# The two attention-gate blocks as a Strassen pair, with P1 and P2 of a layer's first two pairs ahead of its token sums

## The chip, the core and the metric

One core of a Trainium2 chip. The metric is the device time of one execution in microseconds; three executions of the kernel before took 1616.82, 1615.01 and 1616.28 us, median 1616.28. TensorE (PE in the profile) multiplies, VectorE (DVE) and ScalarE (ACT) do elementwise work, GpSimd (POOL) a few small operations and the stores, and SyncE (SP) issues the loads.

## The reference

Two layers of a hybrid encoder on 512 tokens of width 2048, all in float32:

```python
h = rmsnorm(x, g_pre)
z = h @ w_in                       # 2048 -> 7184 columns
gq, gk, gv, gg, ga, aq, ak, av, ag = split_columns(z)
log_a = log_sigmoid(ga @ w_alpha + b_alpha) / 16
o_gla = rmsnorm(gla_chunk_causal(gq, gk, gv, log_a), g_gla) * silu(gg)
o_att = rmsnorm(chunk_band_attention(aq, ak, av, rel_bias), g_att) * silu(ag)
y = concatenate([o_gla, o_att]) @ w_out
x = x + rmsnorm(y, g_post)
```

`ag` and `gg` are the gates of the attention heads and of the GLA heads, 1024 columns each.

## The kernel before

**Products.** The weights lie in HBM as 18 blocks of 512 columns a layer (14 of `w_in`, four of `w_out`); a block is eight chunks of 128x1024 (two k-tiles of 128 rows by 512 columns). One chunk with its product is a `Job`. Every operand is split into a rounded high and a low part, and a product is high·high + high·low + low·high, so three matmuls. `Job.high` casts the chunk to `wh` on ACT (line 221), `Job.low` subtracts on DVE to get `wl` (line 226). The ring of `wh` has four buffers, that of `wl` three: DVE can be three jobs ahead of PE.

`std_gemm` (line 324) uses one chunk for all four token tiles: 24 matmuls of 128x512. `fast_gemm` (line 360) does a pair of blocks by seven Strassen-Winograd products P1 to P7, each on half of the tokens, half of the depth and one block's width: 28 jobs of 12 matmuls, 336 where two blocks by `std_gemm` take 384. The products need sums of weight chunks (DVE, lines 210, 213, 232) and sums of token operands: with A11, A12 (tokens 0 to 255, first and second half of the depth) and A21, A22 (tokens 256 to 511), S1 = A21-A22, S2 = S1-A11, S3 = A11-A21, S4 = A12+S2. P1 takes A11, P2 takes A12, P5 takes S1, P6 S2, P3 S4, P7 S3, P4 A22. `token_sums` makes the sums chunk by chunk, four 128x512 sums and four splits a chunk (lines 648 and 109/110), into four staging slots, stores them to HBM on the POOL queue, and each pair loads them again as `sa` (a ring of four).

**Order of a layer.** AG0 and AG1 (attention gate) by `std_gemm`; then the pairs GG (GLA gate), AV, QK01/QK23, QK45/QK67, GK/GQ, GV; then the output projection, two blocks standard and two as a pair (`W23`, `end=True`) whose P1 and P2 come first with P2 in its own PSUM banks. In layer 1 AG0 runs twice: tokens 0 to 255 first (lines 842 to 845), since the second half of the tokens is finished only after layer 0's last products, and then 256 to 511. Beside the products a list of tasks (`pump`, `Pace`) puts the rest into the program: preparing tokens, their norms, the sums.

**Preparing tokens.** `prep_chunk` scales a chunk of a half's tokens by `g_pre` (ACT/DVE lines 606 to 610) and splits it (109/110); in layer 1 PE first transposes it (593). `token_norms` sums the squares of the token rows on ACT (481), reduces on DVE (482), takes the power on POOL (468), and PE turns the result (549). In layer 0 the rows come from `x` on the SP queue (`load_row`, 500), behind weights and transposed columns; gates need them only at their evacuation. The kernel hands all this to a scheduler, which fixes the order on each engine; an engine takes its instructions in that order.

Of the kernel before, what the change touches and what calls it, by code (L numbers as in the profile page):

```python
# [16 lines left out]
P = 128  # L17
# [3 lines left out]
W = 512  # L21
# [14 lines left out]
def hybrid_trunk(  # L36
# [91 lines left out]
    CO = (0, 4, 1, 5, 2, 6, 3, 7)  # L128
    OO = (5, 4, 7, 6, 2, 3, 0, 1)
    PAIRS = ((GG0, GG1), (AV0, AV1), (QK01, QK23), (QK45, QK67), (GK, GQ), (GV0, GV1))  # L130
# [11 lines left out]
    PROD_END = products(C_END, "P1", "P2", "P5")  # L142
    PROD_END += middle(C_END) + products(C_END, "P7", "P4")
# [7 lines left out]
    class Job:  # L151
# [8 lines left out]
        def load(self):  # L160
# [3 lines left out]
            if k == "std":  # L164
                i = done["load"]
                if i == 0:
                    self.raw = rtile("raw")
                    load_columns(i, 0)
                    parts = w[self.l, b0, c].rearrange("p (k n) -> p k n", k=2)
                    for kk in range(2):  # L170
                        with tc.issue_after(last_load[0]):
                            last_load[0] = nc.sync.dma_start(self.raw[:, kk, :], parts[:, kk, :]).ins
                    load_columns(i, 1)
                elif i < NCH:
                    load_columns(i, 0)
                    self.raw = self.fetch(rtile("raw"), b0, c)
                    load_columns(i, 1)
                    if i == 1:
                        load_gate_columns(0)
                else:  # L180
                    self.raw = self.fetch(rtile("raw"), b0, c)
                if NCH - 2 <= i < NCH + 2:
                    half, j = divmod(i - NCH + 2, 2)
                    with tc.issue_after(last_load[0]):
                        rows[half, j] = load_row(half, j, x, nc.sync)
            elif k == "P1":
                p["H", c] = self.fetch(rtile("H"), b0, top)
            elif k == "P5":
                p["r", c] = self.fetch(rtile("raw"), b1, top)
            elif k == "P6":  # L190
                p["r", c] = self.fetch(rtile("raw"), b1, bottom)
            elif k == "P7":
                p["r", c] = self.fetch(rtile("raw"), b0, top)
            elif k == "P2" or k == "P4" and end:
                p["r", c] = self.fetch(rtile("raw"), b0, bottom)
            src = (so_d if end else sa_d)[self.l].get((LEFT.get(k), c))
            if src is not None:
# [4 lines left out]
        def high(self):  # L202
# [3 lines left out]
            else:  # L206
                h, r = p["H", c], p.get(("r", c))
                src = h if k in ("P1", "P5", "P6", "P4") else r
                if k in ("P5", "P6") or k == "P4" and self.b0 == W23[0]:
# [13 lines left out]
        def low(self):  # L223
# [6 lines left out]
            if self.kind == "P2" and self.b0 != W23[0]:  # L230
# [4 lines left out]
    for l in range(L):  # L235
        for _ in range(min(l, 1) + 1):
            stream += [Job(l, "std", c, AG0) for c in CO]
        stream += [Job(l, "std", c, AG1) for c in CO]
        for b0, b1 in PAIRS:
            pr = {}  # L240
# [3 lines left out]
        pr = {}  # L244
# [113 lines left out]
    roles = ["XY", "YX"]  # L358

    def fast_gemm(l, pair, consume, rate=0.0, skip=0, feature_major=False, after=None, end=False, scaled=True):  # L360
        b0 = pair[0]
        acc = {n: [ps_mm.tile([P, W], F32, tag="mm", name=nm("mm")) for _ in range(2)] for n in roles[0]}
        roles.reverse()
        target = {"P1": "X", "P5": "Y", "P6": "X", "P3": "Y", "P7": "X", "P2": "Y", "P4": "X"}
        starts = ["P1", "P5", "P2"]
        if end:
            target.update(P2="Z", P4="Y")
            starts.append("P4")
        prod = PROD_END if end else PROD
# [25 lines left out]
        def finished(k, t):  # L395
# [9 lines left out]
            elif k == "P4":  # L405
                consume(0, 1, t, x_, None)
# [1018 lines left out]
```

## Time and profile before

| | us |
|---|---|
| median of three runs | 1616.28 (1615.01 to 1616.82) |
| span of the profiled execution | 1614.0 |
| PE busy | 1604.6 (99%) |
| DVE busy | 1213.3 (75%) |
| ACT busy | 897.0 (56%) |
| bytes moved | 469.93 MB, 291 GB/s over the span |
| first product of the GG pair in layer 0 | at 99.3 |

The page gives the profiled execution by its span alone, from the first to the last instruction; 1614.0 is 2.3 under the median, and what lies around it is not shown. Time is worth something where PE would wait: a busy share of 75% on DVE is a mean over stages of which some leave it no slack. A duration in a row is longer than the distance between starts when an engine overlaps one instruction with the next.

### The profile page before, as it was taken

To read this page: it belongs to the slowest core of one execution; us is meant where nothing else is said; L and a number is where in the kernel's file an instruction comes from. 1 tells how busy PE (TensorE), PEld (TensorE's weight loads), DVE (VectorE), ACT (ScalarE), POOL (GpSimd) and SP (SyncE) were. 2 spreads that over 40 slices of the span, in tenths; PEclk is the share of its full clock that TensorE was granted. 3 is DMA by queue.
4 is the path that set the end of the run, shared out by engine and by line. 5 is a ranking of instruction groups with operands and counts; after the bars stand their busy time and mean duration, and the time that the engine had idled before them with its cause. 6 is when DMAs were issued, how large, how long until landed. Compare 5 with 4: busy or idle time off the path is not lost.

```text
span 1614.0 us, 24639 instructions
## 1 busy us (share of the span) xinstructions
PE 1604.6 (99%) x8914; PEld 1372.8 (85%) x8914; DVE 1213.3 (75%) x1566; ACT 897.0 (56%) x1492; POOL 164.2 (10%) x258
## 2 busy tenths in 40 slices
PE   9999999999999999999999999999999999999997
PEld 6888889999988877788888888899999888777886
DVE  7567776787877776678877676768778768866887
ACT  7545544457676534555774445445566765445553
POOL 1210000001101101310122100000001011013100
PEclk9999999999999999999999999999999999999999
DMA  9989786958868698998789897968588676979986
GB/s 373 357 296 335 274 319 221 312 179 292 297 215 292 209 345 284 339 361 304 284 299 341 301 331 268 319 226 300 183 314 294 212 271 235 360 239 353 370 304 236
DMA packets 150809, 469.93 MB, mean 291 GB/s; under 512 B 16444, under 2 KB 35524, under 8 KB 150688
## 3 DMA queue, kind: packets, MB, share of 16 engines
q1 hardware_dynamic: 128096, 390.05, 69.4%
q0 software_dynamic: 22016, 77.37, 12.4%
q8 instruction: 70, 1.15, 0.3%
q10 hardware_dynamic: 576, 0.95, 0.2%
q14 instruction: 51, 0.42, 0.1%
HBM read 396.16 MB, written 71.06 MB: 289 GB/s over the span
## 4 chain that ended last, share of the span: by engine, by line
PE 99%; DMA 0%; DVE 0%; ACT 0%; SPq 0%; DVEq 0%; POOLq 0%; issue 0%
PE mm L430 46%; PE mm L344 22%; PE mm L420 20%; PE ax L937 2%; PE ax L430 1%; PE ax L920 1%; PE ax L1103 1%; PE ax L1137 1%; PE ax L900 1%; PE ax L899 1%; PE ax L898 1%; PE ax L579 1%; PE ax L968 0%; PE ax L593 0%; PE ax L1165 0%; DMA raw<-in_w_dram 0%
## 5 line engine op out<-in xcount | busy, mean ns | idle before, releaser
L430 PE MATMUL mm<-wh,sa 128*128 128x512 f32 x1536 | 483.9, 391 | 0.0
L221 ACT CAST wh<-raw 128x1024 fp32r<-128x1024 f32 x255 | 268.9, 1056 | 246.0 <-PE mm L430 96.9
L226 DVE TENSOR_TENSOR wl<-raw,wh 128x1024 fp32r<-128x1024 f32 (+1 forms) x257 | 312.4, 1218 | 116.9 <-PE mm L430 36.3
L226 DVE TENSOR_TENSOR wl<-H,wh 128x1024 fp32r<-128x1024 f32 x224 | 273.4, 1222 | 117.4 <-PE mm L430 52.3
L221 ACT CAST wh<-H 128x1024 fp32r<-128x1024 f32 x224 | 234.9, 1052 | 216.9 <-PE mm L430 110.5
L430 PEld LDWEIGHTS mm<-wh,sa 128*128 128x128 f32 x1536 | 287.4, 188 | 60.4 <-issue 1.5
L430 PE MATMUL mm<-wl,sa 128*128 128x512 f32 x768 | 299.7, 390 | 0.0
L420 PE MATMUL mm<-sa,wh 128*128 128x256 f32 x1280 | 237.4, 286 | 0.0
L420 PEld LDWEIGHTS mm<-sa,wh 128*128 128x128 f32 x1280 | 199.8, 191 | 0.3
L430 PE MATMUL mm<-wh,a 128*128 128x512 f32 x576 | 187.2, 393 | 0.0
L420 PE MATMUL mm<-sa,wl 128*128 128x256 f32 x640 | 180.6, 283 | 0.0
L430 PEld LDWEIGHTS mm<-wl,sa 128*128 128x128 f32 x768 | 144.2, 188 | 29.7
L344 PE MATMUL mm<-wh,a 128*128 128x512 f32 x512 | 166.4, 393 | 0.1
L210 DVE TENSOR_TENSOR H<-H,raw 128x1024 f32<-128x1024 f32 x120 | 145.6, 1220 | 3.3 <-DMA raw<-in_w_dram 1.7
L468 POOL TENSOR_TENSOR sm<-sm,mhalf 128x4 f32<-128x4 f32 (+2 forms) x40 | 55.1, 1376 | 760.8 <-DVE sm L953 527.6
L430 PEld LDWEIGHTS mm<-wh,a 128*128 128x128 f32 x576 | 107.9, 188 | 24.7 <-issue 2.9
L420 PEld LDWEIGHTS mm<-sa,wl 128*128 128x128 f32 x640 | 122.3, 191 | 0.1
L344 PEld LDWEIGHTS mm<-wh,a 128*128 128x128 f32 x512 | 96.2, 188 | 21.9 <-issue 1.2
L430 PE MATMUL mm<-wl,a 128*128 128x512 f32 x288 | 112.5, 391 | 0.0
L344 PE MATMUL mm<-wl,a 128*128 128x512 f32 x256 | 100.7, 394 | 0.0
L420 PE MATMUL mm<-a,wh 128*128 128x256 f32 x512 | 94.9, 285 | 0.0
L344 PE MATMUL mm<-wh,sa 128*128 128x512 f32 x256 | 86.4, 397 | 0.0
(207 smaller groups left out, 2262.3 us busy)
## 6 DMA issues: line engine op xcount, KB each, us to landing
raw<-in_w_dram SPq DMA_DIRECT2D x319, 512.0 KB, 5.4
sa<-S SPq DMA_DIRECT2D x192, 512.0 KB, 4.8
H<-in_w_dram SPq DMA_DIRECT2D x56, 512.0 KB, 4.4
sa<-A SPq DMA_DIRECT2D x48, 512.0 KB, 6.7
S<-g POOLq DMA_DIRECT2D x32, 512.0 KB, 7.5
oS<-g POOLq DMA_DIRECT2D x32, 512.0 KB, 6.4
sa<-oS SPq DMA_DIRECT2D x32, 512.0 KB, 4.4
sg<-t POOLq DMA_DIRECT2D x32, 256.0 KB, 6.0
```

The costliest lines, as they stand in the source:

```text
L210: nc.vector.tensor_tensor(out=h, in0=h, in1=r, op=ALU.add)
L221: last_cast[0] = nc.scalar.copy(self.wh, src).ins
L226: last_low[0] = nc.vector.tensor_tensor(out=self.wl[:, kk, :], in0=self.src[:, kk, :], in1=self.wh[:, kk, :].bitcast(F32), op=ALU.subtract ...
L344: mm = nc.tensor.matmul(pss[o], a[:, part, t], rhs[:, kk, :], start=(i == 0 and kk == 0 and m == 0), stop=(i == n - 1 and kk == 1 and m == 2),
L420: nc.tensor.matmul(dst, lhs[:, kk, f], a[:, part, tok], start=(fresh and kk == 0 and m == 0 and ft % 2 == 0), stop=(c == c_last and kk == ...
L430: nc.tensor.matmul(out_ps[t], a[:, part, tok], rhs[:, kk, :], start=(fresh and kk == 0 and m == 0), stop=(c == c_last and kk == 1 and m == ...
L468: return nc.gpsimd.tensor_tensor(out=out_r, in0=v, in1=mhalf[:, : v.shape[-1]], op=ALU.pow).ins
L579: mm = nc.tensor.matmul(gate_ps[l][g : g + 32, half * 256 : (half + 1) * 256], gate_w[l][:, kh * 8 + c * 2 + kk, :], full[half, c][:, kh, ...
L898: nc.tensor.matmul(ps[:, :n], self.qh[:, t], self.kh[:, :n], start=True, stop=False)
L899: nc.tensor.matmul(ps[:, :n], self.qh[:, t], self.kl[:, :n], start=False, stop=False)
L900: nc.tensor.matmul(ps[:, :n], self.ql[:, t], self.kh[:, :n], start=False, stop=True)
L937: nc.tensor.matmul(o, self.pt[i][:, j * P : (j + 1) * P], av[hd // 4, j // 2][:, j % 2, (hd % 4) * P : (hd % 4 + 1) * P], start=(j == 0), ...
```

## The change

AG0 and AG1 become a pair of 28 jobs. In each layer the first 16 jobs are P1 and P2 of the AG pair and P1 and P2 of the GG pair, which need only tokens 0 to 255; then come the other five products of AG (20 jobs, 16 of them with a weight chunk of their own to load) and of GG. Both pairs give P2 PSUM banks of its own and start P4 afresh in the second pair of banks (`early`). AG reads the token sums straight from their staging slots, now eight, in the order in which it uses them; GG and later pairs load them from HBM. GG loads its P1 chunks a second time for P5. A21 is no longer split, as nothing reads it. In layer 0 the columns of tokens 0 to 255 are loaded with the first eight jobs, the other half with jobs 8 to 11, the rows of `x` with jobs 5, 7, 12 and 14.

```diff
-        for _ in range(min(l, 1) + 1):
-            stream += [Job(l, "std", c, AG0) for c in CO]
-        stream += [Job(l, "std", c, AG1) for c in CO]
+        infos = [{"early": True, "direct": True}, {"early": True, "second": True}]
+        for (b0, b1), pr in zip(FRONT, infos):
+            stream += [Job(l, k, c, b0, b1, pr) for k, c in early_head(C_IN)]
+        for (b0, b1), pr in zip(FRONT, infos):
+            stream += [Job(l, k, c, b0, b1, pr) for k, c in early_rest(C_IN)]
...
+            elif k == "P1" and p.get("second"):
+                p["r", c] = self.fetch(rtile("raw"), b0, top)
...
             elif k == "P5":
+                if p.get("second"):
+                    p["H", c] = self.fetch(rtile("H"), b0, top)
                 p["r", c] = self.fetch(rtile("raw"), b1, top)
...
-            elif k == "P2" or k == "P4" and end:
+            elif k == "P2" or k == "P4" and p["early"]:
                 p["r", c] = self.fetch(rtile("raw"), b0, bottom)
...
-            if src is not None:
+            if src is not None and (k == "P4" or not (p and p.get("direct"))):
...
-    STAGE = ("g16", "g17", "g4", "g5")
+    STAGE = ("g16", "g17", "g4", "g5", "g6", "g7", "g9", "g10")
...
+    def load_first(i):
+        if 0 < i < 8:
+            load_columns(0, HALF0[i])
+        elif 8 <= i < 12:
+            for ch in HALF1[2 * (i - 8) : 2 * (i - 7)]:
+                load_columns(1, ch)
...
+        if i in (5, 7, 12, 14):
+            half, j = divmod((5, 7, 12, 14).index(i), 2)
+            with tc.issue_after(last_load[0]):
+                rows[half, j] = load_row(half, j, x, nc.sync)
...
+            while not end and len(held) >= len(tags) and held[-len(tags)] not in spent:
+                yield
...
     def token_sums(l):
-        return make_sums(l, False, STAGE, lambda c: (full[0, c][:, 0, :], full[0, c][:, 1, :], full[1, c][:, 0, :], full[1, c][:, 1, :]))
+        order = products(C_IN, "S1") + [({"P6": "S2", "P3": "S4"}[k], c) for k, c in middle(C_IN)]
+        order += products(C_IN, "S3")
...
         if l:
-            std_gemm(l, AG0, (0, 1), CO, operand_in, gate_evac(1, 0), rate=1.2)
             tasks.append(gate_step())
-            tasks.append(token_sums(l))
-            std_gemm(l, AG0, (2, 3), CO, operand_in, gate_evac(1, 0), rate=0.8)
-        else:
-            tasks.append(token_sums(l))
-            std_gemm(l, AG0, range(NT), CO, operand_in, gate_evac(1, 0), rate=1.0, lag=2)
-        std_gemm(l, AG1, range(NT), CO, operand_in, gate_evac(1, 1), rate=1.3, lag=2)
+        tasks.append(token_sums(l))
+        front = [
+            Pair(l, FRONT[0], gate_consume(1), early=True, scaled=False, direct=True, y_banks=aux_banks),
+            Pair(l, FRONT[1], gate_consume(0), early=True, scaled=False),
+        ]
+        for pair in front:
+            pair.run(early_head(C_IN), rate=2.0)
+        front[0].run(early_rest(C_IN), rate=1.0)
         drain()
         tasks.append(forget_gate())
-        fast_gemm(l, PAIRS[0], gate_consume, rate=0.25)
+        front[1].run(early_rest(C_IN), rate=0.25)
```

Three places show how instructions move. First, PE in layer 0, where it turns the norms of tokens 256 to 511 (`ax_627`; `norm` is what POOL made). Before, this stands at the end of AG0, behind eight chunks on all four token tiles:

```order
L344 MATMUL mm_256<-wl_648,sa_504 128x512
L344 MATMUL mm_256<-wh_581,sa_504 128x512
L549 MATMUL ax_627<-cst,norm_208 2x128
L344 MATMUL mm_758<-wh_650,a_21_265 128x512
L344 MATMUL mm_758<-wl_740,a_21_265 128x512
```

After, it stands behind the twelfth job, P1 of the GG pair on its last chunk, and ahead of that pair's P2 (`ax_704`, `ax_705`):

```order
L453 MATMUL mm_562<-wh_527,a_36_329 128x512
L453 MATMUL mm_562<-wl_575,a_36_329 128x512
L453 MATMUL mm_562<-wh_527,a_36_329 128x512
L586 MATMUL ax_671<-cst,norm_208 2x128
L453 MATMUL ax_704<-wh_577,a_37_334 128x512
L453 MATMUL ax_704<-wl_609,a_37_334 128x512
```

It moved from behind 192 matmuls to behind 144. Second, the SP queue in layer 0, where the rows of `x` for these norms (`bias`, `sg`) are loaded; `raw` and `H` are weight chunks. Before, ten chunks stand ahead of the last row:

```order
L157 DMA raw_518<-in_w_dram 128x1024
L500 DMA g_62_520<-in_x_dram 128x1024
L500 DMA g_63_521<-in_x_dram 128x1024
L157 DMA raw_583<-in_w_dram 128x1024
L500 DMA bias_585<-in_x_dram 128x512
L500 DMA bias_586<-in_x_dram 128x512
L500 DMA sg_587<-in_x_dram 128x512
L500 DMA sg_588<-in_x_dram 128x512
```

After, fifteen chunks and `w_alpha` stand ahead of it:

```order
L759 DMA g_115_676<-in_w_alpha_dram 98x512
L164 DMA raw_529<-in_w_dram 128x1024
L525 DMA g_81_531<-in_x_dram 128x1024
L525 DMA g_82_532<-in_x_dram 128x1024
L164 DMA raw_579<-in_w_dram 128x1024
L164 DMA raw_613<-in_w_dram 128x1024
L525 DMA bias_615<-in_x_dram 128x512
L525 DMA bias_616<-in_x_dram 128x512
L525 DMA sg_617<-in_x_dram 128x512
L525 DMA sg_618<-in_x_dram 128x512
```

So five chunks and `w_alpha` have moved ahead of the last row. Third, DVE in layer 1 where the token sums are made (lines 648/683 the sums, 110 their low parts, 226/227 low parts of weights, 211 sums of weight chunks, 401 a gate's combination). Before, they stand between low parts of AG1's chunks, one for 24 matmuls:

```order
L110 TENSOR_TENSOR g_1677_8441<-g_1624_8181,g_1677_8441 128x512
L226 TENSOR_TENSOR wl_8559<-raw_8489,wh_8533 128x1024
L648 TENSOR_TENSOR g_1624_8181<-g_1624_8181,H_7826 128x512
L110 TENSOR_TENSOR g_1678_8452<-g_1624_8181,g_1678_8452 128x512
L648 TENSOR_TENSOR H_7826<-H_7826,g_1624_8181 128x512
L226 TENSOR_TENSOR wl_8585<-raw_8512,wh_8561 128x1024
L110 TENSOR_TENSOR g_1682_8475<-g_1624_8181,g_1682_8475 128x512
```

After, the same sums stand between the low parts of P5 and P6, one for 12 matmuls, each with a sum of weight chunks besides:

```order
L227 TENSOR_TENSOR wl_8667<-H_8124,wh_8641 128x1024
L211 TENSOR_TENSOR H_8068<-H_8068,raw_8672 128x1024
L683 TENSOR_TENSOR g_1718_8414<-g_1718_8414,g_1619_7961 128x512
L110 TENSOR_TENSOR g_1773_8685<-g_1700_8330,g_1773_8685 128x512
L211 TENSOR_TENSOR H_8104<-H_8104,raw_8734 128x1024
L683 TENSOR_TENSOR g_1613_7933<-g_1613_7933,g_1693_8293 128x512
L110 TENSOR_TENSOR g_1764_8646<-g_1693_8293,g_1764_8646 128x512
L401 TENSOR_TENSOR t_1771_8679<-ax_8577,ev_8569 128x512
L110 TENSOR_TENSOR g_1774_8690<-g_1613_7933,g_1774_8690 128x512
L683 TENSOR_TENSOR g_1616_7944<-g_1616_7944,g_1707_8367 128x512
L227 TENSOR_TENSOR wl_8708<-H_8159,wh_8670 128x1024
```

The sums moved from beside products that need one low part in 24 matmuls to beside products that need a low part and a sum in 12.

More of the change, by code (lines that the diff above doesn't have):

```diff
@@ L357, in hybrid_trunk @@
     A = {}
[L358 to L369, printed above, removed]
-        c_first, *_, c_last = C_END if end else C_IN
-        pace = Pace(rate, skip)
-        keep = {}
-        def copies(name, src):
-            keep[name] = []
+    S_on = {}
@@ L595, in prep_chunk @@
                     )
-            if kh == 0:
-                h_end = next(i for i, z in enumerate(stream) if z.l == l - 1 and z.b0 == W23[0] and z.kind == "P4")
-                while half == 0 and done["low"] < min(h_end + 1 + c, len(stream)):
-                    yield
+            if kh == half:
                 full[half, c] = full_tile(half, c)
```

300 lines of the change are left out of this document (165 added, 135 removed).

## The prediction

> **What bounds the kernel now.** I read the page first, then the windows of single stages, then the start of layer 0 instruction by instruction. Page, busy time and the chain that ended last:
>
> ```profile
> PE 1604.6 (99%) x8914; PEld 1372.8 (85%) x8914; DVE 1213.3 (75%) x1566; ACT 897.0 (56%) x1492; POOL 164.2 (10%) x258
> ...
> PE 99%; DMA 0%; DVE 0%; ACT 0%; SPq 0%; DVEq 0%; POOLq 0%; issue 0%
> ```
>
> PE is the path from end to end, so a matmul less is time less, as long as nothing else is late. What one is worth shows where PE does nothing but 128x512 matmuls. Windows (length, then busy time and count of PE, PEld, DVE, ACT, POOL, then granted clock, DMA share, GB/s):
>
> ```profile
> 99.00:175.00 76.00, 76.00 (x337) 62.92 (x336) 58.91 (x56) 38.18 (x44) 4.91 (x9) 1.00 0.89 311
> ```
>
> 76.00 / 337 = 0.2255 us a matmul. A job of a pair (12 matmuls on one weight chunk) takes 2.706, a std job (24) twice that. DVE is busy 78% of this stretch and DMA 89%: there is little room for more of either per matmul, and that is what the change asks for. The start is already full of transfers:
>
> ```profile
> 10.00:20.00 10.00, 10.00 (x56) 7.55 (x56) 9.90 (x18) 9.20 (x16) 0.70 (x1) 1.00 1.04 405
> 20.00:30.00 10.00, 10.00 (x58) 6.68 (x60) 7.93 (x15) 8.27 (x16) 1.50 (x4) 1.00 1.03 405
> 30.00:40.00 10.00, 10.00 (x55) 7.90 (x48) 6.39 (x11) 8.13 (x15) 1.72 (x3) 1.00 1.03 409
> 40.00:50.00 10.00, 10.00 (x57) 7.47 (x56) 6.95 (x14) 6.96 (x17) 3.46 (x8) 1.00 1.04 378
> ```
>
> From 10 to 50 us the DMA share is 1 and the rate about 405 GB/s; PE is nevertheless never idle.
>
> **The matmuls.** Each layer loses 48 matmuls of 128x512 (16 std jobs of 24 become 28 of 12), two layers 96: 96 x 0.2255 = **-21.65 us**. This is the whole gain, if PE stays fed.
>
> **The norms in layer 0, the largest cost.** PE's norm transpose of tokens 256 to 511 needs rows of `x`, their squares, a POOL power and a DVE product. Before, this is how the last rows were issued on SP's queue, when they landed, and how ACT squared them:
>
> ```profile
> L500 SPq DMA_DIRECT2D sg<-in_x_dram x2: 328/328/328, 35.0 to 36.2; - x2
> ...
> DMA to landing us min/median/max: 9.6/10.9/11.1
> ...
> L481 ACT ACTIVATE t<-sg x2: 616/616/616, 47.7 to 48.3; 128x512 bf16<-128x512 f32 x2
> L481 ACT ACTIVATION_READ_ACCUMULATOR t<-sg x2: 188/188/189, 48.3 to 48.9; 128x1 f32 x2
> ```
>
> Then, in the timeline, the reduction, the power, and DVE's copy of the transposed norms:
>
> ```profile
> 49.16 0.16 DVE L482 TENSOR_REDUCE sm<-sm 128x1 f32<-128x5 f32 x1 [1.23 <-ACT t L481]
> 49.40 0.73 POOL L468 TENSOR_TENSOR norm<-sm,mhalf 128x2 f32<-128x2 f32 x1 [0.65 <-DVE sm L482]
> 55.94 0.28 DVE L551 COPY t<-ax 2x128 f32<-2x128 f32 x1 [4.82 <-PE ax L549]
> ```
>
> The last row landed at 36.2 + 9.6 = 45.8, the power ended at 50.13, and PE came to the transpose only at about 55.7: DVE waited for PE, not PE for the norm. Now 15 chunks and `w_alpha` stand ahead of that row instead of ten, 2.83 MB more by the order, at 0.405 MB/us 7.0 us: it lands at 52.8. Behind it come square, accumulate, reduction, power and product, 0.62 + 0.19 + 0.16 + 0.73 + about 0.3 = 2.0 at least, 4.3 as before: the transpose can run at 54.8 to 57.1; I take 55.5.
>
> When is PE there? Its first rows, one group of the gate's small products, and the first GG product, in the timeline and (last) the matmuls by line:
>
> ```profile
> 1.18 4.45 PE L700 MATMUL ax<-t 128*128 128x512 bf16 x10 [1.18 <-DVE t L697]
> 5.07 1.18 PE L344 MATMUL mm<-wh,a 128*128 128x512 f32 x2
> 12.18 0.64 PE L579 MATMUL ax<-g,ev 128*32 128x256 f32 x8
> ```
>
> ```profile
> L430 PE MATMUL mm<-wh,a x32: 388/389/395, 99.3 to 110.9; 128*128 128x512 f32 x32
> ```
>
> Before, 384 matmuls (86.6) and 64 gate products (eight groups like this one, of which I count 0.61, the last one's end overlapping: 4.9) make 91.5 of the 94.2 us from 5.07 to 99.3, so 2.7 was lost at the start; I keep that. After, the transpose stands behind 144 matmuls: 5.07 + 32.5 + 4.9 + 2.7 = 45.2. PE, which executes in order, stands at line 586 from 45.2 to 55.5: **+10** (8 to 12; nothing if rows land 10 us earlier than I think). Queued behind it on PE is P2 of GG, which needs no norm; on DVE the product of the norm and then the copy wait too, ahead of the weight sums and low parts of the next jobs.
>
> **The clock after that stall.** The only long idle of PE in this trace is the end:
>
> ```profile
> 1600.00:1605.00 5.00, 5.00 (x24) 4.14 (x23) 2.22 (x4) 0.69 (x2) 0.56 (x1) 1.00 0.00 0
> 1605.00:1610.00 5.00, 0.96 (x5) 0.45 (x3) 4.18 (x8) 0.69 (x2) 0.54 (x1) 1.00 0.68 267
> 1610.00:1614.00 4.00, 0.00 (x0) 0.00 (x0) 0.47 (x2) 0.00 (x0) 0.00 (x0) 0.51 0.59 191
> ```
>
> The last matmul ends at 1605.96; the granted clock is 1.00 in that window and 0.51 in the next, so more than 4 us of idle halves it. The price is read at the start: ten warm-up matmuls took 4.45 instead of 10 x 0.2255 = 2.26, so **+2.2** (0 to 2.2). The Trainium skill ("TensorE: Matmul & The Clock Gate", section "Why this matters for your kernels") says to leave no PE gap over about 3 us between bursts, since an idle window brings the half clock back; the rows of the end agree, and an estimate from its 3.4 us of warming up would be 1.7 us.
>
> **DVE in the rest of AG.** Distances between starts on DVE in a full stretch:
>
> ```profile
> 853.82 0.67 DVE L110 TENSOR_TENSOR g<-g,g 128x512 fp32r<-128x512 f32 x1
> 854.42 1.21 DVE L226 TENSOR_TENSOR wl<-raw,wh 128x1024 fp32r<-128x1024 f32 x1
> 855.56 0.67 DVE L648 TENSOR_TENSOR g<-g,H 128x512 f32<-128x512 f32 x1
> ```
>
> 0.60 for 128x512, 1.14 for 128x1024. In layer 0, the first combination (line 401) waits for the end of GG's P2. From there to the low part of job 22 the order has 10 instructions of 128x1024 (low parts and weight sums) and 13 of 128x512: 11.4 + 7.8 = 19.2. PE needs that low part after six jobs, 16.2: **+3** (0 to 8). In layer 1, from the low part of job 13 to that of job 22, there are 17 of the large and 30 of the small (token sums, their low parts, two combinations): 19.4 + 18.0 = 37.4 against nine jobs, 24.4. DVE falls back 13.0; the ring of low parts lets it be three jobs ahead, 8.1: **+4.9** (0 if sums run earlier, 13 without lead).
>
> **GG's rest and its transfers.** GG's five other products now load P1's chunks again. The nearest stage of before is the same five products of a later pair:
>
> ```profile
> 727.00:782.00 55.00, 55.00 (x245) 45.53 (x244) 48.88 (x51) 28.50 (x40) 4.12 (x7) 1.00 0.88 318
> ```
>
> There 36 loads at 318 GB/s cost PE nothing. After, 40 loads of 0.524 MB and about 1.6 MB of the gate's stores fall in 54.1 us: 22.6 MB, 418 GB/s, over the 409 shown. At 409 it is 55.3 us, 1.2 late; and three jobs of lead, 8.1 us, do not cover a landing of 9.6 to 10.9 as in the full stretch above. I take **+2 in each layer, +4** (0 to 14, the upper end if every landing is late).
>
> **What costs nothing.** ACT gets ten copies a layer at this price (form of 128x512, by lines):
>
> ```profile
> L381 ACT COPY ev<-mm 128x512 f32<-128x512 f32 x40 | 23.3, 584 | 19.3 <-PE mm L420 12.3 <-PE mm L430 7.0
> ```
>
> 5.8 us on an engine that is idle half of the 76 us window; without that cover it would cost its 5.8. The 16 added weight sums and 12 or 4 added low parts are in the DVE counts; the four splits of A21 that go free 2.4 us of DVE there.
>
> **Sum.** 1614.0 - 21.65 + 10 + 2.2 + 3 + 4.9 + 4 = 1616.5 of span; the median of the runs lies 2.3 over this span: 1618.8, say **1619**.
>
> **The rivals.** A measurement here tells about 0.2%, 3.2 us, from no change: 1613.0 to 1619.5.
>
> *The forecast:* the gain is eaten by waits that the closer packing exposes. 1619, 1612 to 1629 by the terms' bounds. Chance 0.55, of which 0.04 faster, 0.24 within 0.2%, 0.27 slower. Its weakest term is the norm wait, which rests on one rate.
>
> *The norm is there in time:* if those rows land by about 43, the 12.2 fall away and the rest stands: 1606.5, faster. For it: the rate of 378 from 40 to 50 shows that the queue begins to empty; against it: three windows at 405 to 409 with fewer chunks ahead. Chance 0.20.
>
> *DVE stays ahead:* the scheduler's rows are counted as if DVE were always busy, but its waits may lie elsewhere; then 7.9 fall away: 1610.9. For it: DVE stands at 78% in the widest stretch without costing PE anything; against it: 37.4 for 24.4 is an excess of 53%, which no lead of three jobs absorbs. Chance 0.13, of which 0.02 within 0.2%.
>
> *Transfers bound layer 0's whole front:* slower. By the order 66.8 MB lie ahead of GG's last chunk; PE needs 56 jobs, 151.5 us, from 5.07. At 405 GB/s they take 165, which the norm and DVE waits already cover; at the 378 of the last window 176.7, so 20.1 in place of the 10, 3 and one 2 there: 1618.8 + 5.1 = 1624. It decides below 66.8 MB / (151.5 + 5.1 + 15) us = 390 GB/s. Chance 0.12. The Trainium skill ("HBM Reference", the section on its specifications) gives about 358 GB/s as a core's share and about 425 for a core that streams alone; the windows at 405 speak for the second, and an estimate by the first would be some 10 us slower still.
>
> **How the numbers follow.** Faster: 0.04 + 0.20 + 0.11 = 0.35. Same: 0.24 + 0.02 = 0.26. Slower: 0.27 + 0.12 = 0.39. The range reaches down to the norm rival, 1605, and up to 1629; outside are the cases in which two rivals hold at once (1598.6) and the worst transfers, about 0.18 together. Cases of both signs are in it; the forecast's own range is 1612 to 1629.
>
> **What would show it.** Right: 96 matmuls fewer; one idle of PE of 8 to 12 us ahead of line 586 between 44 and 57 us, ended by POOL's norm, with the granted clock under 1 just behind; idle of PE ahead of line 453 ended by a low part of line 227 in AG's P5 and P6 of both layers; a DMA share of 1 and small waits for `sa` in GG's rest. Wrong: no idle at line 586 (then the rows came earlier), or DVE's rows idle while PE runs on, or PE waiting for `raw` from the first jobs on (then the transfers bind).

## The result, and the profile after

The changed kernel takes 1643.7 us (median of four, 1638.2 to 1644.9) where the kernel before took 1616.6 beside it: 1.0164 times as long, 95% interval 1.0148 to 1.0180. It is 27 us slower. Run again with other kernels it took 1641.3, 1.0159 times (1.0143 to 1.0175). Its profiled execution has a span of 1636.4 us and is the quickest of its runs, so the losses counted below are some 5 us short of the median's.

The page, busy time and the chain that ended last:

```profile
PE 1598.3 (98%) x8818; PEld 1354.3 (83%) x8818; DVE 1270.3 (78%) x1626; ACT 918.3 (56%) x1520; POOL 165.8 (10%) x258
...
PE 88%; DMA 5%; DVE 3%; ACT 2%; issue 1%; SPq 0%; DVEq 0%; POOL 0%; POOLq 0%; ACTq 0%
```

There are 96 matmuls fewer, and a tenth of the chain is no longer PE's own. DVE has 57 us more to do. What PE waited for, over the whole execution (us in total, times, longest):

```profile
PE ax L586 <- POOL norm L493: 7.5, 2, 5.9
PE mm L453 <- ACT wh L222: 5.6, 7, 1.2
PE ax L453 <- DVE wl L227: 5.6, 3, 2.9
PE mm L453 <- DMA sa<-A: 2.1, 3, 1.0
PE mm L453 <- DVE wl L227: 2.1, 3, 1.1
PE mm L453 <- ACT a L109: 1.6, 1, 1.6
```

Before, this view has one row, of 1.2 us at the start. The transpose of the norms leads the list; then come casts and low parts of chunks (`wh`, `wl`) and operands (`sa`), in many small pieces. The layers share the damage: before, the first transpose of the attention (line 920, after the change line 957) stands at 325.7 and the last at 1343.5; after:

```profile
L957 PE MATMUL ax<-cst,t x160: 270/272/329, 339.4 to 1365.7; 128*128 128x128 f32 x160
```

Layer 0 is 13.7 us later and layer 1 adds 8.5. With the 10.8 that the matmuls of each layer no longer need, 24.5 us were lost in layer 0 and 19.3 in layer 1.

To place them, I took the starts of all PE instructions, the distance from each to the next, and from it the usual distance of its kind (the median of its form), and added what is over by stretch of the program. It counts waits, matmuls at half clock and changes between kinds of matmul. The 64 gate products of a layer start almost together and are counted too, some 3 to 6 us in any kernel.

| lost us | 0–60 | 60–110 | 110–220 | 800–860 | 860–930 | 930–1040 |
|---|---|---|---|---|---|---|
| what runs there after | layer 0, P1 and P2 of both pairs | AG's P5, P6, P3 | rest of AG, GG's rest | output product, P1 and P2 | AG's P5, P6, P3 | rest of AG, GG's rest |
| before | 6.2 | 0 | 0 | 4.0 | 0 | 0 |
| after | 18.9 | 4.0 | 7.4 | 4.6 | 11.8 | 6.5 |
| after, run again | 19.0 | 4.4 | 8.7 | 6.7 | 12.4 | 8.3 |

A column can change because the gate products move. In layer 1 they run at 846.4 to 849.7 us before, at 861.7 to 865.0 after and at 865.6 to 868.9 in the run after that. Their 3 us stand in 800–860 before and in 860–930 after, so some 8.5 of after's 11.8 belong to AG, and all of its 4.6 to the end of layer 0's output product and the products behind it.

Windows of layer 0 after (columns as in the prediction):

```profile
40.00:60.00 20.00, 14.05 (x66) 8.71 (x65) 11.68 (x20) 10.73 (x20) 2.32 (x5) 0.83 1.03 410
60.00:70.00 10.00, 10.00 (x45) 8.21 (x45) 7.60 (x10) 3.14 (x4) 0.56 (x1) 1.00 0.92 351
70.00:80.00 10.00, 8.95 (x37) 6.26 (x35) 10.00 (x14) 6.75 (x10) 2.14 (x4) 1.00 0.76 266
80.00:90.00 10.00, 9.04 (x36) 6.52 (x36) 10.00 (x14) 6.67 (x10) 2.67 (x5) 1.00 0.63 222
...
120.00:130.00 10.00, 10.00 (x46) 8.10 (x44) 8.26 (x10) 4.72 (x7) 1.08 (x2) 1.00 1.02 412
130.00:140.00 10.00, 7.98 (x33) 5.88 (x33) 9.47 (x9) 5.54 (x7) 0.54 (x1) 1.00 1.03 414
...
180.00:190.00 10.00, 9.29 (x39) 6.74 (x38) 5.72 (x5) 3.04 (x4) 0.00 (x0) 1.00 1.03 413
190.00:200.00 10.00, 8.95 (x39) 6.77 (x38) 6.76 (x8) 7.07 (x8) 1.08 (x2) 1.00 1.02 409
```

Three stages follow each other. To 60 us the transfers are full and PE stands at the norm. From 70 to 90 DVE is full (10.00 of 10) and the transfers fall to 222 GB/s, where before they moved 370. From 120 the transfers are full again in most windows, at 404 to 414 (285 and 364 from 150 to 170), and PE waits in small pieces. SP's queue waited from 60 to 110 us for this:

```profile
SPq L164 <- DVE wl L227: 32.9, 8, 9.4
SPq L164 <- DVE H L211: 12.3, 3, 5.5
```

The load of a chunk (line 164) waits for a buffer, and the buffer for DVE's low part or sum of an earlier chunk. A late DVE can thus stop the loads of the next stage. These waits alone don't show that it does: before, the queue waited 40.6 us in this stretch, 32.8 of them for DVE, while the transfers went on at 348 GB/s (309 after). The run with less work on DVE, below, bears on it.

In layer 1 DVE is full from 870 to 900, and ACT before that, at the end of layer 0's output product:

```profile
810.00:820.00 10.00, 7.11 (x28) 4.46 (x26) 5.26 (x11) 10.00 (x22) 1.80 (x3) 1.00 0.26 82
...
870.00:880.00 10.00, 8.36 (x36) 6.26 (x34) 10.00 (x13) 4.74 (x6) 1.59 (x3) 1.00 0.87 289
880.00:890.00 10.00, 8.06 (x33) 6.04 (x33) 10.00 (x14) 7.08 (x11) 2.14 (x4) 1.00 0.78 315
890.00:900.00 10.00, 7.87 (x27) 6.30 (x28) 10.00 (x13) 5.24 (x9) 3.20 (x6) 0.83 0.65 223
```

The longest wait there, 2.94 us, ends with the low part (line 227) in the last of these rows of DVE:

```profile
887.87 0.67 DVE L683 TENSOR_TENSOR g<-g,g 128x512 f32<-128x512 f32 x1
888.48 0.67 DVE L110 TENSOR_TENSOR g<-g,g 128x512 fp32r<-128x512 f32 x1
889.08 0.67 DVE L401 TENSOR_TENSOR t<-ax,ev 128x512 f32<-128x512 f32 x1
889.68 0.67 DVE L110 TENSOR_TENSOR g<-g,g 128x512 fp32r<-128x512 f32 x1
890.27 0.67 DVE L683 TENSOR_TENSOR g<-g,g 128x512 f32<-128x512 f32 x1
890.88 1.20 DVE L227 TENSOR_TENSOR wl<-H,wh 128x1024 fp32r<-128x1024 f32 x1
```

### The profile page after: what moved, and what is told of

Its sections match the earlier page's. It is cut to its first block, busy times and chain, and to the rows that moved or that the text cites. A ratio compares the mean times of both kernels' runs of the same rounds, so it can differ in the third digit from the quotient of the medians.

```text
span 1636.4 us, 24588 instructions
## 1 busy us (share of the span) xinstructions
PE 1598.3 (98%) x8818; PEld 1354.3 (83%) x8818; DVE 1270.3 (78%) x1626; ACT 918.3 (56%) x1520; POOL 165.8 (10%) x258
## 4 chain that ended last, share of the span: by engine, by line
PE 88%; DMA 5%; DVE 3%; ACT 2%; issue 1%; SPq 0%; DVEq 0%; POOL 0%; POOLq 0%; ACTq 0%
PE mm L453 44%; PE mm L443 20%; PE mm L347 10%; PE ax L453 6%; PE ax L974 2%; DMA raw<-in_w_dram 2%; DMA H<-in_w_dram 2%; DVE wl L227 1%; PE ax L957 1%; PE ax L1140 1%; DMA sa<-A 1%; PE ax L1174 1%; DVE H L211 1%; PE ax L936 1%; PE ax L937 1%
## 5 line engine op out<-in xcount | busy, mean ns | idle before, releaser
L453 PE MATMUL mm<-wh,sa 128*128 128x512 f32 x1536 | 486.3, 392 | 4.5 <-DMA sa<-A 2.1
L227 DVE TENSOR_TENSOR wl<-H,wh 128x1024 fp32r<-128x1024 f32 (+1 forms) x249 | 302.6, 1218 | 107.0 <-PE mm L453 40.3
L227 DVE TENSOR_TENSOR wl<-raw,wh 128x1024 fp32r<-128x1024 f32 x248 | 303.0, 1223 | 105.2 <-PE mm L453 31.2
L453 PE MATMUL mm<-wh,a 128*128 128x512 f32 x576 | 189.4, 397 | 5.1 <-ACT wh L222 3.5
L211 DVE TENSOR_TENSOR H<-H,raw 128x1024 f32<-128x1024 f32 x152 | 184.6, 1220 | 10.3 <-DMA raw<-in_w_dram 6.6
L453 PEld LDWEIGHTS mm<-wh,a 128*128 128x128 f32 x576 | 106.9, 188 | 34.3 <-ACT wh L222 5.7
L453 PE MATMUL mm<-wl,a 128*128 128x512 f32 x288 | 112.6, 393 | 1.6 <-DVE wl L227 1.6
L347 PE MATMUL mm<-wh,a 128*128 128x512 f32 x256 | 82.8, 393 | 0.0
L443 PEld LDWEIGHTS mm<-a,wh 128*128 128x128 f32 x512 | 80.3, 191 | 0.2
L214 DVE TENSOR_TENSOR raw<-H,raw 128x1024 f32<-128x1024 f32 x64 | 78.2, 1221 | 2.1 <-DMA raw<-in_w_dram 1.6
L443 PE MATMUL mm<-a,wl 128*128 128x256 f32 x256 | 72.4, 283 | 0.0
```

The lines of the kernel that those rows point to most:

```text
L211: nc.vector.tensor_tensor(out=h, in0=h, in1=r, op=ALU.add)
L214: nc.vector.tensor_tensor(out=r, in0=h, in1=r, op=ALU.subtract)
L227: last_low[0] = nc.vector.tensor_tensor(out=self.wl[:, kk, :], in0=self.src[:, kk, :], in1=self.wh[:, kk, :].bitcast(F32), op=ALU.subtract ...
L347: mm = nc.tensor.matmul(pss[o], a[:, part, t], rhs[:, kk, :], start=(i == 0 and kk == 0 and m == 0), stop=(i == n - 1 and kk == 1 and m == 2),
L443: nc.tensor.matmul(dst, lhs[:, kk, f], a[:, part, tok], start=(fresh and kk == 0 and m == 0 and ft % 2 == 0), stop=(c == self.last and kk ...
L453: nc.tensor.matmul(out_ps[t], a[:, part, tok], rhs[:, kk, :], start=(fresh and kk == 0 and m == 0), stop=(c == self.last and kk == 1 and m ...
```

## The experiments

My first theory was that of the prediction: separate waits that add up. The rival is its fourth case, widened: DVE and the transfers bound the fronts as a whole, so that a wait taken away alone comes back further on. Times are medians, with the ratio to the kernel before run beside each.

**The transpose of the second norms moved away.** In layer 0 it comes after the token sums are emitted:

```diff
+        normed.add((l, half))
+        if (l, half) != (0, 1):
+            turn_norms(l, half)
+        yield
+
+    def turn_norms(l, half):
+        r = norm[l][:, 0, 2 * half : 2 * half + 2]
         ps = aux()
         nc.tensor.transpose(ps[0:2, 0:P], r, ident)
...
         tasks.append(token_sums(l))
+        if l == 0:
+            tasks.append(turn_late())
...
```

> Layer 0's transpose of the second norms runs behind the token sums instead of ahead of GG's P2; the norms themselves stay where they are on DVE. Theory (PE stood in order at a wait that nothing behind it needed): the idle of 5.9 us and the nine matmuls at half clock behind it (1.8) go, DVE's wait for POOL stays and gives back up to half: 4 to 8 us off the changed kernel. Rival (the transfers bound the front as a whole, so a wait taken away comes back as a wait for the next chunks): 0 to 2 us off.

Measured: 1640.7, 1.0152 (1.0137 to 1.0168), 1 to 2 us off by the ratios, with intervals that overlap. The losses of layer 0 went from 18.9, 4.0, 7.4 to 11.2, 7.0, 12.0: together 30.3 before the edit (32.1 in the second run of the changed kernel) and 30.2 behind it. The first stretch won 7.7, and the other two lost about as much. Its waits from 110 to 215 us:

```profile
PE mm L453 <- DMA sa<-A: 3.5, 3, 1.9
PE mm L453 <- DMA sa<-S: 2.9, 2, 2.6
PE mm L453 <- ACT wh L222: 1.5, 3, 0.7
```

PE came there earlier and waited for operands instead. The rival holds: in layer 0 the long wait at line 586 is the visible one, but to take it away alone gains little or nothing.

**GG without the second load of P1's chunks.** P5 adds to what AG left in its tile, so GG's values are no longer the right ones, and only the time counts:

```diff
-                    p["H", c] = self.fetch(rtile("H"), b0, top)
+                    p["H", c] = infos_of[self.l]["H", c]
```

> GG's P5 adds its chunk to the sum that AG left instead of loading P1's chunk again, so four loads (2.1 MB) a layer are left out and GG's values are others; DVE, ACT and PE do the same work. Theory (GG's rest asks for more than the transfers give, its waits are late chunks and late operands): 2.1 MB at 0.409 MB per us are 5.1 us of transfers a layer against 3.8 and 5.2 us of waits there: 5 to 9 us off in both layers together. Rival (ACT's casts, which most of these waits name, are late for their own sake): 0 to 2 us off.

Measured: 1635.5, 1.0124 (1.0108 to 1.0140), some 6.5 us off by the ratios, as the theory expected. 110 to 220 lost 5.6 (7.4), 930 to 1040 3.8 (6.5). The transfers matter, but 4 of 40 loads do not free the stage.

**Layer 1's first sums with the columns.** Gate products and S1 of a chunk follow its columns:

```diff
             yield from prep_chunk(l, half, ch, xs)
+            if half and ch < 4:
+                gate_products(l, (ch,))
+                sums_of.setdefault(l, token_sums(l))
+                while (l, False, "S1", ch) not in made:
+                    next(sums_of[l])
+                    yield
```

> In layer 1 the gate products and the first token sum of a chunk are made as soon as its columns are ready, not behind all columns and both norms, so some of the DVE work of 870 to 900 us moves into the time before 862, in which DVE idles half. Theory (DVE bounds AG's P5 and P6 in layer 1): four sums and four low parts, 8 x 0.60 = 4.8 us, come earlier, 4 to 7 us off with the half clock that goes too. Rival (the chunks of these products land late): 0 to 1 us off.

Measured: 1640.8, 1.0152 (1.0137 to 1.0167). 860 to 930 lost 8.7 (11.8), but 800 to 860 lost 9.4 (4.6) and 930 to 1040 9.3 (6.5). No gain that can be told from none: a miss for the theory. The shift itself is small: some 2 us of it are gate products that the edit puts ahead of 860, and the unaltered kernel's second run loses 6.7 and 8.3 in the two columns that grew.

**The token sums on POOL.**

```diff
-                nc.vector.tensor_tensor(out=out, in0=in0, in1=in1, op=op)
+                (nc.vector if end else nc.gpsimd).tensor_tensor(out=out, in0=in0, in1=in1, op=op)
```

> The 16 token sums of a layer (128x512) run on POOL, which is busy 10%, instead of DVE. Theory (DVE bounds): DVE has 16 x 0.60 = 9.6 us less in each layer; layer 1 gains 6 to 9, layer 0 some 2: 8 to 11 us off, if POOL makes a sum in less than about 1.5 us. Rival (POOL is slow enough, or holds DVE up enough, to be the late one itself): no gain, or slower.

Measured: 1656.9, 1.0244 (1.0218 to 1.0270), slower by 13. POOL's sums take 1.3 us (median of 24) against 0.67 on DVE, and DVE is held up meanwhile. DVE's low parts of chunks from 862 to 912 us, by lines; then one low part of a sum and what POOL did beside it, in the timeline:

```profile
L227 DVE TENSOR_TENSOR wl<-H,wh 128x1024 fp32r<-128x1024 f32 x3 | 9.5, 3158 | 0.0
```

```profile
880.78 5.43 DVE L110 TENSOR_TENSOR g<-g,g 128x512 fp32r<-128x512 f32 x1 [1.70 <-ACT g L109]
```

```profile
880.66 1.30 POOL L683 TENSOR_TENSOR g<-g 128x512 f32<-128x512 f32 x1
881.92 1.28 POOL L683 TENSOR_TENSOR g<-g,g 128x512 f32<-128x512 f32 x1
883.16 1.28 POOL L683 TENSOR_TENSOR g<-g 128x512 f32<-128x512 f32 x1
884.40 1.25 POOL L683 TENSOR_TENSOR g<-g,g 128x512 f32<-128x512 f32 x1
```

In the changed kernel the same took DVE 1208 and 674 ns in the mean. Here the low part of the sum began at 880.78, just behind the start of the first of POOL's four sums, and ended at 886.21, 0.56 us behind the last of them. An idle engine is no help if its work stops the busy one. The Trainium skill ("SBUF — State Buffer", section "SBUF: two separate sides") says that DVE with two SBUF inputs and GpSimd lock one pair of ports against each other for a whole instruction; the 5.43 us agree with it.

**Less for DVE, less to load, and all at once.** The changed kernel ran again (second row of the table above) beside three others: one without DVE's low parts of the token sums, in whose place ACT copies the sum once more; one in which GG reads AG's last four staged sums instead of loading its own; and one with both and the late transpose. These three leave out work that the result needs, and only their time counts. The two edits:

```diff
-                split(op[:, 0, :], op[:, 1, :], src)
+                if end:
+                    split(op[:, 0, :], op[:, 1, :], src)
+                else:
+                    nc.scalar.copy(op[:, 0, :], src)
+                    nc.scalar.copy(op[:, 1, :], src)
```

```diff
-            if src is not None and (k == "P4" or not (p and p.get("direct"))):
+            if src is not None and (k == "P4" or not (p and p["early"] and not end)):
...
-            return S_on[self.l, LEFT[k], c]
+            return S_on[self.l, LEFT[k] if self.direct else "S3", c]
```

> The changed kernel once more, unaltered, so that the others of this call stand beside it on the same chip: 1640 to 1645.

> The low parts of the 16 token sums of a layer are not subtracted on DVE; ACT copies the sum a second time in their place, so values are others, loads and stores the same. DVE has 9.6 us less a layer. Theory (DVE bounds AG's P5 and P6, and frees the chunk buffers late there, so that the transfers idle and then pile up in GG's rest): the losses of 862 to 930 us in layer 1 (11.7) fall to 3 or less, those of layer 0 from 60 to 110 (4.0) go, and those in GG's rest fall by some 3 in each layer: 12 to 18 us off. Rival (GG's rest is bound by its own transfers, whatever stands ahead): only the DVE stretches gain, 8 to 12 off.

> GG's P5, P6, P3 and P7 read the four S3 tiles that AG left in the staging slots instead of loading their sums, so 16 loads (8.4 MB, 20 us of transfers at 409 GB/s) a layer are left out and GG's values are others. Theory (transfers bound GG's rest): its losses (7.4 in layer 0, 6.5 in layer 1) all but go, the other stretches keep theirs: 10 to 14 us off. Rival (casts and low parts of the chunks are late there for want of ACT and DVE): under 4 off.

> The late transposes of the norms, the token sums without low parts on DVE and GG on staged sums, all three. Theory (the lost time is the norms' wait, DVE in AG's rest and transfers in GG's, and each gave back to the next when it was taken away alone): together they free what each alone did not, layer 0's loss falls from 30 to about 13 and layer 1's from 23 to about 8: 30 to 34 us off, below the kernel before. Rival (something else paces the fronts): the sum of the single gains or less, 20 to 25 off.

| lost us | time | ratio (95%) | 0–60 | 60–110 | 110–220 | 800–860 | 860–930 | 930–1040 |
|---|---|---|---|---|---|---|---|---|
| after, run again | 1641.3 | 1.0159 (1.0143–1.0175) | 19.0 | 4.4 | 8.7 | 6.7 | 12.4 | 8.3 |
| DVE less | 1634.7 | 1.0115 (1.0092–1.0139) | 18.9 | 2.6 | 5.3 | 6.2 | 7.6 | 7.4 |
| 16 loads less | 1625.9 | 1.0062 (1.0047–1.0077) | 19.4 | 4.2 | 1.7 | 7.4 | 9.6 | 0 |
| all three | 1619.7 | 1.0024 (1.0013–1.0035) | 11.1 | 5.3 | 2.6 | 10.0 | 3.8 | 0 |

The loads are the largest single cause: 15.4 us go with them (10 to 14 expected), and GG's rest loses only 1.7 and 0. Its windows without them, and the changed kernel's:

```profile
110.00:215.00 105.00, 103.83 (x456) 85.22 (x455) 86.16 (x81) 55.72 (x64) 7.10 (x13) 1.00 0.80 294
...
930.00:1020.00 90.00, 90.00 (x399) 74.50 (x398) 72.08 (x67) 47.78 (x55) 4.92 (x9) 1.00 0.76 278
```

```profile
110.00:215.00 105.00, 100.27 (x432) 79.95 (x431) 83.83 (x79) 54.75 (x63) 6.98 (x13) 1.00 0.95 360
...
930.00:1020.00 90.00, 85.29 (x370) 68.53 (x369) 70.70 (x67) 45.44 (x55) 5.99 (x11) 1.00 0.96 362
```

In one stretch of layer 1, 399 matmuls in 90 us instead of 370, at a DMA share of 0.76 instead of 0.96. The edit takes away the bytes of these loads and also their places in SP's queue, and no run separates the two. From 110 to 215 us the queue waited 28.5 us for PE to free a buffer for a sum in the changed kernel, but 46.9 us in the kernel before, where PE lost nothing; that speaks for the bytes.

DVE's part is smaller, 6.6 us, less than either the theory (12 to 18) or its rival (8 to 12) expected. Of the lost us, 3.4 lie in layer 0's stretch from 110 to 220, behind the one in which the sums are made. That fits the buffers' way from DVE to the loads, and so does the stretch from 60 to 110, with DVE's work as it is and with less of it:

```profile
60.00:110.00 50.00, 47.98 (x203) 37.52 (x202) 47.25 (x56) 28.83 (x39) 9.63 (x18) 0.99 0.84 310
```

```profile
60.00:110.00 50.00, 48.76 (x210) 39.09 (x210) 40.47 (x43) 37.34 (x56) 10.77 (x20) 0.99 0.91 333
```

Taken together, the edits left 1619.7, 21.6 us off, not the 1608 to 1611 that I had expected; the rival on record for this run, 20 to 25 off, holds. The single gains (1 to 3, 6.6 and 15.4) add up to little more. Losses of 11.1 and 10.0 stayed in the two heads, the first stretch of each layer (6.2 and 4.0 before). With the loads and DVE's work gone, the late transpose kept what it won: 0 to 60 loses 8 us less, and 60 to 220 loses 7.9, as much as with DVE's work alone gone (7.9) and 2 more than with the loads alone gone (5.9).

**A version that loads the sums once.** The runs pointed to an order in which the two pairs take turns, so that a staged sum serves both before its slot is filled again. The sums spread over 40 jobs instead of 20, and GG's 16 loads of sums and 4 of A22 go; nothing that the result needs is left out. The stream and the use of a slot:

```diff
-        for (b0, b1), pr in zip(FRONT, infos):
-            stream += [Job(l, k, c, b0, b1, pr) for k, c in early_rest(C_IN)]
+        for k, c in shared_rest(C_IN):
+            stream += [Job(l, k, c, b0, b1, pr) for (b0, b1), pr in zip(FRONT, infos)]
...
-            spent.add((self.l, LEFT.get(k), c))
+            if self.b0 != AG0:
+                spent.add((self.l, LEFT.get(k), c))
```

Besides, four staging slots become GG's weight tiles, both pairs keep P5 and P3 in `aux` banks, and the forget gate follows the rest, with layer 0's transpose of the second norms. A second kernel binds each token sum behind the low part ahead of it in the program, a third adds the early sums of layer 1, and a fourth has this binding alone on the changed kernel:

```diff
-            with tc.issue_after(last_state[0]) if end else nullcontext():
+            with tc.issue_after(last_state[0] if end else last_low[0]):
```

> The two pairs take turns in their five other products: each token sum is staged once and used by AG and then GG before its slot is filled again, so GG's 16 loads of sums and 4 of A22 fall away and the sums are made over 40 jobs instead of 20; the second norms' transpose comes after the rest. The computation is complete. Theory (DVE in AG's rest and transfers in GG's rest are the two bounds): the transfers of the rest fall by 10.5 MB a layer, its losses in the later half go, the DVE work is the same but spread: 1610 to 1622. Rival (DVE, with 40 jobs in which all sums come first, stands as full as before): 1625 to 1635.

> As the one that takes turns, with each sum bound behind the low part that stands ahead of it in the program, so that DVE doesn't make sums early while low parts wait. Theory (DVE's order in the first ten jobs of the rest sets what is lost there): 3 to 8 us under the one without it. Rival (only DVE's total counts): the same within 2.

> As the paced one, and in layer 1 gate products and first sums start with the columns. Theory: 2 to 5 us under the paced one in layer 1, and the fastest of all, 1603 to 1613. Rival (layer 1's head is full on ACT and takes it back): within 2 of the paced one.

> The changed kernel with only this binding of sums behind low parts; work and loads unaltered. Theory (in AG's rest PE waits for low parts that stand behind sums nobody needs yet): the loss of 862 to 930 us in layer 1 falls from 12 to 5 to 8, layer 0's GG rest gains 1 to 3 as chunk buffers come free sooner: 4 to 8 us off. Rival (DVE has too much work there in any order): 0 to 2 off.

| lost us | time | ratio (95%) | 0–60 | 60–110 | 110–220 | 800–860 | 860–930 | 930–1040 |
|---|---|---|---|---|---|---|---|---|
| taking turns | 1624.8 | 1.0056 (1.0041–1.0071) | 12.1 | 11.0 | 0 | 9.3 | 9.9 | 0 |
| and paced | 1618.0 | 1.0013 (1.0003–1.0022) | 12.7 | 9.2 | 0 | 9.6 | 1.5 | 0 |
| and early sums | 1620.7 | 1.0028 (1.0017–1.0038) | 14.1 | 9.4 | 0 | 10.1 | 3.6 | 0 |
| pacing alone | 1640.3 | 1.0145 (1.0123–1.0167) | 19.0 | 3.4 | 9.2 | 2.9 | 7.4 | 7.9 |

Taking turns, with these moves, is worth 17 us and empties both of the stretches in which GG's rest lay, as expected; its time is above the 1610 to 1622 expected, and 60 to 110 us now loses 11.0 (4.4). Pacing then takes 6.8 us more, as expected. Of the 8.4 that 860 to 930 wins by it, some 3 are gate products, which now run ahead of 860. On the changed kernel pacing gives layer 1 the expected stretch (12.4 to 7.4, in an execution of 1635.0 us, 5.3 under the median) and no time that can be told from none. Both fit one lesson, which they don't prove: DVE's order pays only where the transfers behind it are free. The early sums gave nothing, against the expectation (2.6 us slower, with intervals that overlap).

**What was left of it.** Three steps on the paced kernel: all norm transposes behind the rest; layer 0's gate products in one piece (`gate_step` in both layers); GG's chunks of P1 loaded once in layer 0. Then the last without the second, and the last alone:

```diff
-        if (l, half) != (0, 1):
-            turn_norms(l, half)
...
-            if l == 0:
-                turn_norms(0, 1)
+            for half in range(2):
+                turn_norms(l, half)
...
-                p["r", c] = self.fetch(rtile("raw"), b0, top)
+                if self.l == 0:
+                    p["H", c] = self.fetch(slot(("g6", "g7", "g9", "g10")[c], [2, 512]), b0, top)
+                else:
+                    p["r", c] = self.fetch(rtile("raw"), b0, top)
...
```

> The paced kernel in which the pairs take turns, with all four transposes of the norms behind the rest of the front. Theory (in the tail of layer 0's output product PE stands at a transpose that is needed only by the forget gate, and pays half clock behind it): its 5.7 us there fall to 1 or 2, 2 to 5 us under the paced one (1618.0). Rival (ACT's casts are as late as the norm, the wait only changes its name): within 1 of it.

> Besides, layer 0's 64 gate products stand in one piece behind the columns instead of in groups between the products. Theory (each change between the two kinds of matmul costs PE some 0.1 us, 30 to 50 us lost 8.7 against 2.0 before): 2 to 4 us under the one with late transposes. Rival (the products wait for their columns either way): same within 1.

> Besides, layer 0 loads GG's P1 chunks once, into the tiles that keep them until P4, which the rows of x give up. Theory (from 50 to 95 us layer 0 loses 10 us to chunks that land late behind 405 GB/s of transfers): 2.1 MB less are up to 5 us, 2 to 5 us off, 1606 to 1613 and under the kernel before. Rival (DVE, not the chunks, holds PE in that stretch): same within 1.

> Turns taken and paced, transposes late, GG's chunks loaded once in layer 0, and layer 0's gate products again in groups as the changed kernel has them. Theory (in one piece they hold the first sum back, which cost 5.6 us of waiting and 2.6 of half clock at 66 us): 3 to 7 us under the one with all four edits (1616.9), so 1610 to 1614 and faster than before by 0.1% to 0.4%. Rival (DVE is behind there in any case): the same within 1.5.

> The same with the transposes of the norms where the paced one has them, so only the single load is added to it. Theory (late transposes are worth little, since ACT's casts are as late in layer 1's head): within 2 of the one above, 1611 to 1616. Rival (PE's wait at the transpose costs its 1.6 us and half clock): 3 to 5 above it.

| | time | ratio (95%) |
|---|---|---|
| late transposes | 1618.4 | 1.0013 (1.0003–1.0022) |
| and gate products in one piece | 1618.9 | 1.0019 (1.0010–1.0028) |
| and GG's chunks once in layer 0 | 1616.9 | 1.0002 (0.9991–1.0013) |
| late transposes and chunks once | 1616.1 | 0.9997 (0.9988–1.0006) |
| chunks once alone | 1617.1 | 1.0006 (0.9997–1.0014) |

The late transposes gave nothing, the gate products in one piece nothing: both misses, with the rivals right. To put the gate products back in groups (fourth row) was expected to give 3 to 7 us and gave 0.8, a miss too. The single load gave 1 to 3 us by the ratios, with intervals that overlap. The best of them equals the kernel before, and none beats it by its median. The ten runs of the third row reach from 1613.7 to 1619.6, with none between 1615.0 and 1618.7; what divides them no run here shows.

## Why the prediction was wrong

I forecast 1619 in a range to 1629, 0.15% slower; it is 1.64% slower. By its steps, on the profiled execution:

- **The matmuls** are right: 96 fewer, and with all losses (44 us by the two layers' delays and this gain) it comes out. The forecast's losses were 24.1 us. Of the 20 us more, some 10 stand in GG's rest, 5 in DVE's two terms and 4 in the output product's tail.
- **The norms' wait in layer 0** is right in place and time: the transpose ran at 56.15 (55.5 forecast). PE came at 50.2, not 45.2, since 30 to 50 us lost 8.8, where before it was 2.0 (10 to 30 lost 0.6, where before it was 3.4). Much of it stands at gate products in small groups between the products, though to put them in one piece gained nothing. So the wait was 5.9, not 10. But its meaning was wrong. I added it to the other terms, and the first experiment showed that without it layer 0 loses the same 30 us.
- **The clock** is right in size (1.6 us, forecast 2.2) and wrong in its condition. I wrote that "more than 4 us of idle halves it"; 2.94 us did in layer 1 (below), so it was paid twice.
- **DVE in the rest of AG**: 3 in layer 0 was 4.0. In layer 1 it was some 8.5, half clock included, against 4.9: DVE was full from 862 to 897, and the low part that PE wanted stood behind two token sums, two of their low parts and a combination (the rows above); I had counted a full lead of three jobs and no such order. Pacing recovers most of it in the kernel that takes turns.
- **GG's rest and its transfers** is the step that failed: "I take +2 in each layer, +4". They took 7.4 and 6.5 us, 13.9 where the sum had 4, with DMA at 0.95 and 0.96 of its share, and 15.4 us of the whole kernel's time went with 16 loads a layer. I had the 418 GB/s that this stretch asks for and the 409 that it gets, and priced the difference over the whole stretch, 1.2 us. But the loads come in bursts, after a pause at 222 GB/s that DVE's buffers explain in part, and the shortage is then larger and not made good. That the loads cause the loss is shown by the run without them; that the pause makes it larger is argued from the windows and from the run with less work on DVE.
- **What costs nothing** left out layer 0's output product ahead of layer 1: in the tail PE waits 1.5 us for layer 1's first norm and in short pieces for casts and low parts, 4 us in all that the kernel before did not lose. ACT is full there, 10.00 of 10 from 810 to 820. Before, that norm was ready 2.8 us ahead of PE (POOL ended at 801.40, PE came at 804.18). Why it now comes later against PE wasn't settled.
- **The range** doesn't follow from "the terms' bounds", as I said. The terms at their upper bounds (12, 2.2, 8, 13 and 14) make a median of 1643.9, the measured time, partly by chance; at the lower ones it is 1602.7. To stop at 1629 I took it that they would not go wrong together, and gave no reason. The runs suggest one: the terms are linked through DVE and the transfers.
- **The rivals**: the fourth, transfers that bound layer 0's front, came nearest, but with a chance of 0.12 and as something that comes in place of the forecast's terms, at 1624. It was to decide below 390 GB/s. Full windows ran at 404 to 414, yet the mean from 0 to 215 us was 355, with the pause in it. It holds in both layers, and with DVE, not in place of it.

What stays open is the 5 us by which most runs of the changed kernel exceed its profiled one (the second profiled execution, at 1644.5, loses more in every stretch but the first), and the losses that remain in both heads when GG's loads are gone.

## What to carry to other kernels

A change that takes work from the bound engine makes every transfer and every side engine's instruction denser in time; sum the demand of each stage for each of them, and look for the order in which a pause in one is followed by a burst that it cannot make good. Waits found one by one are not a sum: take one away, and see whether the next moves. Where two products use the same operands, share each while it is staged, which was worth more here than all shifting of waits.

## What the runs showed of the hardware

Half clock comes sooner than the end of the kernel before had suggested. In layer 1, PE waited 2.94 us (timeline):

```profile
892.13 0.50 PE L453 MATMUL ax<-wl,g 128*128 128x512 f32 x1 [2.94 <-DVE wl L227]
```

It idled 2.81 of 3 us, and the next window's granted clock is 0.66 in the mean (windows of the changed kernel):

```profile
889.00:892.00 3.00, 0.19 (x1) 0.00 (x0) 3.00 (x5) 2.47 (x4) 1.61 (x3) 1.00 0.62 243
892.00:897.00 5.00, 4.87 (x14) 3.85 (x15) 5.00 (x7) 1.40 (x2) 0.53 (x1) 0.66 0.45 166
56.00:60.00 4.00, 3.85 (x10) 3.08 (x11) 1.70 (x4) 0.63 (x1) 0.66 (x2) 0.50 1.02 397
```

In the paced kernel no single wait of the output product's tail was over 1.57 us, and the clock halved behind them nonetheless (timeline):

```profile
809.53 0.27 PE L607 MATMUL ax<-cst,norm 128*2 128x128 f32 x1 [1.57 <-POOL norm L506]
810.07 0.73 PE L356 MATMUL mm<-wh,g 128*128 128x512 f32 x2 [0.26 <-ACT wh L230]
811.33 0.50 PE L356 MATMUL mm<-wl,g 128*128 128x512 f32 x1 [0.53 <-DVE wl L235]
...
812.82 0.63 PE L356 MATMUL mm<-wh,g 128*128 128x512 f32 x1
813.25 0.63 PE L356 MATMUL mm<-wl,g 128*128 128x512 f32 x1
```

The last two start 0.43 us apart, twice the usual. Each time seven to nine matmuls ran so, at 0.2 us more each: 1.4 to 1.8 us. The wait of 5.9 us in layer 0 cost no more of this than the 2.94: by the trace's clock records it was half from 53.27 us for 6.83, but PE still stood until 56.15; behind the shorter wait it was half from 892.94 for 3.41.
